# Hybrid decoder trunk on one core: own tiles for the retention's outputs, and raw weights in four slots of 4 KB instead of two of 8 KB

## The chip, the cores and the metric

The kernel runs on one core of a Trainium2 chip. The metric is the device time of one execution in microseconds (us), the median of several runs. The core has five engines with an instruction queue each: TensorE (PE, matmuls; PEld is its weight load), VectorE (DVE), ScalarE (ACT), GpSimd (POOL) and SyncE (SP, which here only issues DMA transfers). SBUF is the on-chip memory with 128 partitions, PSUM the accumulators that matmuls write, in banks of 128 x 512 float32 here. An engine works through its queue in order; between engines an instruction waits on semaphores.

## The reference

Two layers, each with a mixing part of three branches and a gated feed-forward part (FFN), in float32, for one sequence of 512 positions and 1024 channels. Cut to what matters here:

```
for l in range(2):
    h = rmsnorm(x, norm_mix_g[l])
    proj = h @ w_in[l]               # q, k, v of 4 attention heads; q, k, v, g of retention;
                                     # three conv streams; 3 x 1024 gate columns
    o_da  = rmsnorm(diff_attention(q, k, v, lam, bias)) * (1 - lam_init)
    o_ret = rmsnorm(retention(rq, rk, rv)) * silu(r_g)
    o_sc  = sc_b * causal_dwconv(sc_c * sc_x)
    gates = sigmoid(gate_pre + b_gate[l])
    y = gates0 * (o_da @ w_branch_da) + gates1 * (o_ret @ w_branch_ret) + gates2 * (o_sc @ w_branch_sc)
    x = x + y @ w_out[l]
    h = rmsnorm(x, norm_ffn_g[l])
    g_ff, u_ff = split(h @ w_ffn_in[l])          # 2 x 2816
    g_ff = causal_dwconv(g_ff)
    x = x + (silu(g_ff) * u_ff) @ w_ffn_out[l]
```

Differential attention subtracts a second softmax map, times lambda, from the first; a head has two maps of 64 channels each and values of 128.

## The kernel before

**Splitting.** Every float32 product runs as three matmuls of float32r parts (mm3, lines 159 to 161): high x high, high x low, low x high. So each weight tile is loaded raw by SP (load_w, line 137), its high half is made by ACT (line 150) and its low half by DVE (line 151, raw - high). Activations are split in the same way (lines 166 and 167; with a gain on them lines 169 and 170). The raw tiles share one tag of two slots of 8 KB per partition, the high and low halves of wide weights three slots each (HL). A load can be issued once an earlier tile of its slot has been split.

**Mixing.** "natural" computes projections with the positions on PSUM's partitions (four banks, tag "main", per head or pair): pnrqk and pnrvg for retention, pnh0 to pnh3 for the attention heads. "evacuate" (line 430) empties each bank of a head: a copy to nat, a square in place, v by split, a sum to msqk. The gates' and the convolution's projections (wt, tiles hi_t, lo_t; PSUM ptg and ptsc) run with channels on partitions; "gate" and "branch" make one gate and its branch product (pb) for a block d of 128 output channels. These, and the heads' projections, are the generator "filler". "weave" runs the steps of retention and attention and after each step asks the filler for work of a given cost (COVER), so that code order, with the waits for slots, sets the order of each engine's queue.

**Attention head h** makes q and k (transposes pt0, pt1, high and low parts in q, k, klz), then for each of four blocks i of 128 positions: scores (pS0, pS1, lines 487 and 488), bias and row minimum on DVE (line 492), exponential on ACT (493), combine (DVE), turn (transposes pT, line 511, split to aT), values (po, lines 523 and 524, with aT and v). At its end o is normalised, transposed (pto, line 284) and split to om. A name such as pT20L is pT of head 2, block 0; por00L and PT00L are the retention's.

**Slots.** q, k, v, rv, knh, knl, nat, rT, om, omr, y and act share tag "N", nine slots of 4 KB. The pool gives a new tile a free slot. In the program before, v of head 3 (v3) takes the slot of k of head 2 (k2) in both layers, whose last reader is the score matmul pS123. PSUM's main banks are four, shared by the heads' projections, gates, branches and the FFN.

**FFN.** The raw tile of one f (128 gate and 128 up columns) is 1 MB, in four blocks of 512 columns per partition. Group 0 (5 f's, "plain") uses the odd and the even blocks as gate and up weights. The other 17 f's of a layer ("seven") form seven block products in place of eight: fa (high and low of one block), s31 (two sums), s24 (two sums, from s31), fb (two blocks), each split on ACT and DVE, 84 matmuls of 256 columns. "rows" multiplies the group's activations by w_ffn_out (w2, PSUM p2) and adds to x. SP's issues are kept in program order only at the start, until all eight blocks of x are split.

## Time and profile before

| What | Value |
|---|---|
| median of 3 runs | 1548.77 us (1547.65 to 1552.67) |
| the profiled execution | 1550.88 us, span 1549.1 us |
| clock granted to PE, mean | 0.993 |
| PE busy | 1526.5 us (99%) |
| DVE, ACT busy | 1101.2 us (71%), 731.9 us (47%) |
| DMA | 148.54 MB, 96 GB/s over the span |

The span runs from the first to the last instruction of the profile; 1.8 us lie around it in that execution. A row of the timeline has the start in us, the duration, the engine, the line, the operation with its output and inputs, and in brackets the idle time of the engine ahead of it with what ended it. A window's row has, per engine, the busy time and the number of instructions, then the granted clock as a share of full speed, the busy share of the DMA engines and GB/s. Matmuls overlap, so the pace of PE is read from their starts, not from their durations.

### The profile page before, as it was taken

What the parts mean: (1) busy time and instruction counts of PE and PEld (TensorE: products, weight loads), DVE (VectorE), ACT (ScalarE), POOL (GpSimd) and SP (SyncE); (2) the same over time, 40 slices, a digit from 0 to 9 for tenths busy, and PEclk for the clock granted to TensorE, in tenths of its full rate; (3) what the DMA queues carried; (4) which work ended last, traced back from release to release, by engine and by line L of the source; (5) the groups of instructions that cost most, each with busy time, mean ns of one, the idle gap of its engine ahead of it and who ended that gap; (6) DMA issues with size and microseconds to landing.
All of it is one profiled execution on the core that took longest, in us unless ns stands there. A gap on an engine that the chain in (4) does not pass through costs nothing.

```text
span 1549.1 us, 21866 instructions
## 1 busy us (share of the span) xinstructions
PE 1526.5 (99%) x8510; PEld 1345.9 (87%) x8510; DVE 1101.2 (71%) x2040; ACT 731.9 (47%) x1304; POOL 14.1 (1%) x27
## 2 busy tenths in 40 slices
PE   9999989999999999999999999899999999999998
PEld 7899878888887999899789999688888879988997
DVE  7588776655569996597666887665546789957963
ACT  4456555433344564365425565453334446634641
POOL 1000000000000000000100000000000000000000
PEclk9999999999999999999999999899999999999999
DMA  5322222232221332331322222222323132224213
GB/s 188 116 103 63 88 74 84 85 98 96 98 88 55 142 110 69 136 137 55 129 82 92 72 89 72 68 81 90 102 76 123 68 110 110 92 84 165 96 45 106
DMA packets 43287, 148.54 MB, mean 96 GB/s; under 512 B 5703, under 2 KB 6102, under 8 KB 37552
## 3 DMA queue, kind: packets, MB, share of 16 engines
q1 hardware_dynamic: 41328, 143.37, 27.7%
q0 software_dynamic: 1856, 3.77, 0.7%
q8 instruction: 67, 1.10, 0.3%
q14 instruction: 36, 0.29, 0.1%
HBM read 145.01 MB, written 3.42 MB: 96 GB/s over the span
## 4 chain that ended last, share of the span: by engine, by line
PE 92%; DVE 3%; DMA 2%; ACT 2%; issue 1%; SPq 0%; ACTq 0%; DVEq 0%
PE pnrvgL L161 1%; PE pnrvgL L159 1%; PE pnrvgL L160 1%; PE pnrqkL L160 1%; PE pnrqkL L161 1%; PE pnrqkL L159 1%; PE pnh2L L161 1%; PE pnh2L L160 1%; PE pnh2L L159 1%; PE pnh1L L161 1%; PE pnh1L L160 1%; PE pnh1L L159 1%; PE pnh0L L160 1%; PE pnh0L L159 1%; PE pnh0L L161 1%
## 5 line engine op out<-in xcount | busy, mean ns | idle before, releaser
L150 ACT CAST hi_tL<-raw_tL 128x1024 fp32r<-128x1024 f32 x60 | 62.9, 1049 | 135.0 <-DMA raw_tL<-in_wt 18.3
L150 ACT CAST hi_w2L<-raw_w2L 128x640 fp32r<-128x640 f32 (+2 forms) x64 | 49.4, 781 | 97.8 <-DMA raw_w2L<-in_w 49.8
L151 DVE TENSOR_TENSOR lo_tL<-raw_tL,hi_tL 128x1024 fp32r<-128x1024 f32 x60 | 73.4, 1224 | 19.0 <-ACT hi_tL L150 18.8
L151 DVE TENSOR_TENSOR lo_w2L<-raw_w2L,hi_w2L 128x640 fp32r<-128x640 f32 (+2 forms) x64 | 56.2, 889 | 37.8 <-ACT hi_w2L L150 35.7
L150 ACT CAST hi_fbL<-raw_fL 128x1024 fp32r<-128x1024 f32 x34 | 35.7, 1051 | 26.2 <-PE p216L L160 11.7
L150 ACT CAST hi_oL<-raw_oL 128x1024 fp32r<-128x1024 f32 x16 | 16.9, 1054 | 58.1 <-issue 19.5
L151 DVE TENSOR_TENSOR lo_fbL<-raw_fL,hi_fbL 128x1024 fp32r<-128x1024 f32 x34 | 41.6, 1222 | 1.7 <-ACT hi_fbL L150 1.6
L150 ACT CAST hi_faL<-raw_fL 128x512 fp32r<-128x512 f32 x34 | 21.1, 622 | 30.9 <-DMA raw_fL<-in_wf 26.8
L151 DVE TENSOR_TENSOR lo_fuL<-raw_fL,hi_fuL 128x1024 fp32r<-128x1024 f32 x10 | 12.2, 1224 | 19.6 <-ACT hi_fuL L150 19.6
L150 ACT CAST hi_fuL<-raw_fL 128x1024 fp32r<-128x1024 f32 x10 | 10.5, 1051 | 31.2 <-PE pg0L L160 11.0
L151 DVE TENSOR_TENSOR lo_faL<-raw_fL,hi_faL 128x512 fp32r<-128x512 f32 x34 | 23.4, 689 | 0.3
L150 ACT CAST hi_nrvgL<-raw_nrvgL 128x1024 fp32r<-128x1024 f32 x8 | 8.4, 1051 | 31.5 <-PE pnrvgL L161 13.5
L150 ACT CAST hi_fgL<-raw_fL 128x1024 fp32r<-128x1024 f32 x10 | 10.5, 1054 | 24.1 <-issue 9.5
L151 DVE TENSOR_TENSOR lo_oL<-raw_oL,hi_oL 128x1024 fp32r<-128x1024 f32 x16 | 19.6, 1224 | 2.8 <-ACT hi_oL L150 2.8
L151 DVE TENSOR_TENSOR lo_nrvgL<-raw_nrvgL,hi_nrvgL 128x1024 fp32r<-128x1024 f32 x8 | 9.8, 1224 | 12.6 <-ACT hi_nrvgL L150 12.6
L151 DVE TENSOR_TENSOR lo_nh0L<-raw_nh0L,hi_nh0L 128x768 fp32r<-128x768 f32 x8 | 7.7, 958 | 13.4 <-ACT hi_nh0L L150 13.4
L150 ACT CAST hi_nrqkL<-raw_nrqkL 128x1024 fp32r<-128x1024 f32 (+1 forms) x9 | 8.6, 953 | 16.1 <-issue 11.1
L150 ACT CAST hi_bdL<-raw_bdL 128x512 fp32r<-128x512 f32 x16 | 9.9, 618 | 10.7 <-PE pb50L L160 2.2
L151 DVE TENSOR_TENSOR lo_nrqkL<-raw_nrqkL,hi_nrqkL 128x1024 fp32r<-128x1024 f32 (+1 forms) x9 | 9.9, 1105 | 7.0 <-ACT hi_nrqkL L150 7.0
L150 ACT CAST hi_nh0L<-raw_nh0L 128x768 fp32r<-128x768 f32 x8 | 6.7, 838 | 15.4 <-PE pnh0L L161 7.8
L151 DVE TENSOR_TENSOR lo_fgL<-raw_fL,hi_fgL 128x1024 fp32r<-128x1024 f32 x10 | 12.2, 1222 | 2.1 <-ACT hi_fgL L150 2.1
L150 ACT CAST hi_nh3L<-raw_nh3L 128x768 fp32r<-128x768 f32 x8 | 6.7, 835 | 14.0 <-PE ptg17L L160 7.3
(8455 smaller groups left out, 5985.4 us busy)
## 6 DMA issues: line engine op xcount, KB each, us to landing
raw_fL<-in_wf SPq DMA_DIRECT2D x44, 1024.0 KB, 4.8
raw_tL<-in_wt SPq DMA_DIRECT2D x60, 512.0 KB, 3.3
raw_w2L<-in_w SPq DMA_DIRECT2D x32, 320.0 KB, 2.9
raw_oL<-in_wo SPq DMA_DIRECT2D x16, 512.0 KB, 3.3
raw_w2L<-in_w SPq DMA_DIRECT2D x16, 512.0 KB, 3.5
raw_nrvgL<-in_wr SPq DMA_DIRECT2D x8, 512.0 KB, 3.2
raw_bdL<-in_wda SPq DMA_DIRECT2D x16, 256.0 KB, 2.6
raw_w2L<-in_w SPq DMA_DIRECT2D x16, 256.0 KB, 2.6
```

The source lines that it names most:

```text
L150: A.copy(h, raw)
L151: V.tensor_tensor(w, raw, h.bitcast(F32), ALU.subtract)
L159: T.matmul(o, a[0], b[0], start=start, stop=False, skip_group_check=more)
L160: T.matmul(o, a[0], b[1], start=False, stop=False, skip_group_check=more)
L161: T.matmul(o, a[1], b[0], start=False, stop=stop, skip_group_check=more)
```

## The change

Three things. The two outputs of retention, omr0 and omr1, get tiles of their own in the layer's mixing pool instead of slots of tag "N". The raw tag has four slots of 4 KB (16 KB as before). And the FFN's loads are made of two halves: "plain" loads the gate blocks and the up blocks apart, "seven" loads two neighbouring blocks at a time, so that s31's broadcast sum over blocks of both halves becomes two sums of 512 columns. The layout in memory is the same, so a plain half comes in pieces of 2 KB.

```diff
--- before.py
+++ after.py
@@ -131,10 +131,10 @@
         return i
 
     def load_w(src, name):
-        n = src.shape[1]
+        n = int(np.prod(src.shape[1:]))
         with tc.high_priority():
-            raw = wp.tile([P, n], F32, tag="raw", bufs=2, name="raw_" + name, padded_shape=[P, 2 * D])
-            ordered(nc.sync.dma_start(raw, src))
+            raw = wp.tile([P, n], F32, tag="raw", bufs=4, name="raw_" + name, padded_shape=[P, D])
+            ordered(nc.sync.dma_start(raw if len(src.shape) == 2 else raw.rearrange("p (b n) -> p b n", b=src.shape[1]), src))
         return raw
 
     def split_w(raw, name):
@@ -643,7 +643,7 @@
             yield
             yield
             ps = transposes(lambda st: o[:, st * P : (st + 1) * P], f"ptor{p}{L}")
-            om[4 + p] = split2(ps, pairN(f"omr{p}{L}"), pt[:, G_RET : G_RET + 1])
+            om[4 + p] = split2(ps, mp.tile([P, 2, S], F32R, name=f"omr{p}{L}"), pt[:, G_RET : G_RET + 1])
             yield
 
 
@@ -770,9 +770,9 @@
             split(flat(t), flat(X[k][:, 0, 3:7]), flat(X[k][:, 1, 3:7]))
 
         def plain(f):
-            raw = load_w(wf[l, f], f"f{L}{f}").rearrange("p (b n) -> p b n", n=S)
+            both = wf[l, f].rearrange("p (b n) -> p b n", n=S)
             ps = main(f"pg{f}{L}")
-            project(xg, ps, split_w(raw[:, 1::2], f"fg{L}{f}"))
+            project(xg, ps, split_w(load_w(both[:, 1::2], f"fg{L}{f}"), f"fg{L}{f}"))
             if not norm:
                 norm.append(norm_x(f"f{L}")[1])
             padt = pads[f % 2]
@@ -782,20 +782,20 @@
             conv(c, padt, lambda t: pt[:, wc + t : wc + t + 1], pt[:, FF_B + f : FF_B + f + 1])
             A.activation(c, c, AF.Silu)
             ps = main(f"pu{f}{L}")
-            project(xg, ps, split_w(raw[:, 0::2], f"fu{L}{f}"))
+            project(xg, ps, split_w(load_w(both[:, 0::2], f"fu{L}{f}"), f"fu{L}{f}"))
             u = temp(f"u{f}{L}")
             V.tensor_tensor(u, ps, norm[0], ALU.mult)
             V.tensor_tensor(u, u, c, ALU.mult)
             return split2(u, pairN(f"act{f}{L}"))
 
         def seven(f):
-            raw = load_w(wf[l, f], f"f{L}{f}")
-            r4 = raw.rearrange("p (b n) -> p b n", n=S)
-            a11, a12 = r4[:, 1], r4[:, 3]
+            upper, lower = [load_w(wf[l, f, :, b * D : (b + 1) * D], f"f{b}{L}{f}") for b in range(2)]
+            a21, a11, a22, a12 = upper[:, :S], upper[:, S:], lower[:, :S], lower[:, S:]
             with tc.high_priority():
-                w11 = split_w(raw[:, S : 2 * S], f"fa{L}{f}")
+                w11 = split_w(a11, f"fa{L}{f}")
                 s31 = fp.tile([P, 2, S], F32, tag="sum", name=f"s31{f}{L}", bufs=2)
-                V.tensor_tensor(s31, r4[:, 0:1].broadcast_to([P, 2, S]), r4[:, 1:3], ALU.add)
+                V.tensor_tensor(s31[:, 0], a21, a11, ALU.add)
+                V.tensor_tensor(s31[:, 1], a21, a22, ALU.add)
                 h31, l31 = slotX(f"h31{f}{L}"), slotX(f"l31{f}{L}")
                 split(s31, h31, l31)
                 s24 = fp.tile([P, 2, S], F32, tag="sum", name=f"s24{f}{L}", bufs=2)
@@ -803,7 +803,7 @@
                 V.tensor_tensor(s24[:, 1], s24[:, 0], a12, ALU.add)
                 h24, l24 = slotX(f"h24{f}{L}"), slotX(f"l24{f}{L}")
                 split(s24, h24, l24)
-                w2212 = split_w(raw[:, 2 * S : 4 * S], f"fb{L}{f}")
+                w2212 = split_w(lower, f"fb{L}{f}")
             w22, w12 = [tuple(t[:, b * S : (b + 1) * S] for t in w2212) for b in range(2)]
 
             def product(o, w, b, start, stop):
```

The places where the order of instructions differs follow, from the program before and from the changed one.

PE, layer 0, from the end of head 3's projection (pnh3L03 is its fourth bank) on; po02 are the values of head 2, pS0 and pS1 its scores, pto1 head 1's output. Before, pT20 is directly ahead of po02, and nine more rows of head 2 follow the last one shown ahead of pb22, the first branch product:

```order
L161 MATMUL pnh3L03_2044<-hi_nh3L06_2200,xs7mL0_233 128x384
L511 MATMUL pT20L0_2152<-ident_79,s020L0_2030 128x128
L523 MATMUL po02L0_2192<-v2L0_1562,aT20L0_2154 128x256
L524 MATMUL po02L0_2192<-v2L0_1562,aT20L0_2154 128x128
L284 MATMUL pto1L0_2248<-ident_79,o1L0_1543 128x128 x4
L487 MATMUL pS022L0_2257<-k2L0_1934,q2L0_1933 128x384
L488 MATMUL pS022L0_2257<-klzL0_122,q2L0_1933 128x384
L487 MATMUL pS122L0_2258<-k2L0_1934,q2L0_1933 128x384
L488 MATMUL pS122L0_2258<-klzL0_122,q2L0_1933 128x384
L511 MATMUL pT21L0_2271<-ident_79,s021L0_2144 128x128 x2
```

The same place of PE in the changed program; pT20 stands seven rows ahead of the first one shown:

```order
L161 MATMUL pnh3L02_2043<-hi_nh3L06_2200,xs7mL0_233 128x384
L159 MATMUL pnh3L03_2044<-hi_nh3L06_2200,xs6mL0_230 128x384
L160 MATMUL pnh3L03_2044<-lo_nh3L06_2201,xs6mL0_230 128x384
L161 MATMUL pnh3L03_2044<-hi_nh3L06_2200,xs6mL0_230 128x384
L159 MATMUL pnh3L03_2044<-hi_nh3L06_2200,xs7mL0_233 128x384
L160 MATMUL pnh3L03_2044<-lo_nh3L06_2201,xs7mL0_233 128x384
L161 MATMUL pnh3L03_2044<-hi_nh3L06_2200,xs7mL0_233 128x384
L523 MATMUL po02L0_2192<-v2L0_1562,aT20L0_2154 128x256
L524 MATMUL po02L0_2192<-v2L0_1562,aT20L0_2154 128x128
L159 MATMUL pb22L0_2300<-oms0L0_1034,hi_b2L02_2296 128x512
L160 MATMUL pb22L0_2300<-oms0L0_1034,hi_b2L02_2296 128x512
```

So pT20 has 13 matmuls of pnh3 between it and po02, and pb22 follows po02 at once. Behind pb22 come a gate of 24 matmuls, the next branch product and five matmuls of another gate, and only then pto1, pS022 and pS122. Layer 1 has the same order as layer 0 here.

ACT, layer 0, the same stretch. Before, from aT20 up to the first copies into v3 (line 169), which stand behind the exponential s023 of block 3:

```order
L166 CAST aT20L0_2154<-pT20L0_2152 128x128
L433 ACTIVATE pnh3L03_2044<-pnh3L03_2044 128x256
L525 COPY o2L0_2020<-po02L0_2192 128x128
L527 ACTIVATE po02L0_2192,mso2L0_2022<-o2L0_2020,zs2L0_2021 128x128
L493 ACTIVATE s022L0_2263,z22L0_2256<-s022L0_2263,mn022L0_2264 128x384
L493 ACTIVATE s122L0_2267,z22L0_2256<-s122L0_2267,mn122L0_2268 128x384
L166 CAST aT21L0_2274<-pT21L0_2271 128x256
L493 ACTIVATE s023L0_2361,z23L0_2354<-s023L0_2361,mn023L0_2362 128x512
L525 COPY o2L0_2020<-po02L0_2192 128x128
L169 ACTIVATE v3L0_2039<-pnh3L00_2041,rmL0_298 128x128
L169 ACTIVATE v3L0_2039<-pnh3L01_2042,rmL0_298 128x128
```

In the changed program, from the conversion of a gate's weights on:

```order
L150 CAST hi_tL026_2409<-raw_tL026_2407 128x1024
L432 COPY nat3L0_2038<-pnh3L00_2041 128x256
L433 ACTIVATE pnh3L00_2041<-pnh3L00_2041 128x256
L166 CAST aT20L0_2154<-pT20L0_2152 128x128
L169 ACTIVATE v3L0_2039<-pnh3L00_2041,rmL0_298 128x128
L432 COPY nat3L0_2038<-pnh3L01_2042 128x256
L433 ACTIVATE pnh3L01_2042<-pnh3L01_2042 128x256
L169 ACTIVATE v3L0_2039<-pnh3L01_2042,rmL0_298 128x128
```

Each copy into v3 now follows the square of its bank. On DVE the low half of v3 and the sum msqk3 of the first three banks follow aT20's low half, which has one lo_t ahead of it.

SP, at the start. Before, the third load of retention's projection waits behind four constants:

```order
L198 DMA x3_85<-in_xT 128x512
L204 DMA par1_111<-in_par 128x140
L205 DMA gtab_t_113<-in_gtab 128x32
L206 DMA mask_t_90<-in_mask 128x128
L380 DMA ropeL0_126<-in_rope 128x512
L137 DMA raw_nrqkL02_182<-in_wr 128x1024
L198 DMA x4_86<-in_xT 128x512
```

In the changed program it follows x3 at once, and the constants stand behind the last load of that projection:

```order
L198 DMA x3_85<-in_xT 128x512
L137 DMA raw_nrqkL02_182<-in_wr 128x1024
L198 DMA x4_86<-in_xT 128x512
L198 DMA x5_87<-in_xT 128x512
L198 DMA x6_88<-in_xT 128x512
L198 DMA x7_89<-in_xT 128x512
L137 DMA raw_nrqkL04_222<-in_wr 128x1024
```

Over the whole program PE has the same 8510 matmuls, DVE 34 sums more, and SP 44 loads more.

## The prediction

> **What bounds the kernel now.** I read the page's busy shares and its chain first, then the waits of PE, then the granted clock in slices.

> ```profile
> PE 1526.5 (99%) x8510; PEld 1345.9 (87%) x8510; DVE 1101.2 (71%) x2040; ACT 731.9 (47%) x1304; POOL 14.1 (1%) x27
> PE 92%; DVE 3%; DMA 2%; ACT 2%; issue 1%; SPq 0%; ACTq 0%; DVEq 0%
> ```

> PE is on 92% of the chain that ended last, and the change leaves all its matmuls in place. So only time in which PE stands, or runs at a lower clock, can be won. The waits of PE (total, times, longest) name these places:

> ```profile
> PE po02L L523 <- ACT aT20L L166: 3.9, 2, 2.0
> PE pto1L L284 <- DVE o1L L544: 2.7, 2, 1.4
> PE pb22L L159 <- DVE msqk3L L435: 2.2, 2, 1.4
> PE por00L L617 <- ACT PT00L L166: 1.8, 1, 1.8
> PE po02L L524 <- DVE aT20L L167: 1.4, 2, 0.7
> PE pnrqkL L159 <- ACT hi_nrqkL L150: 1.3, 2, 1.1
> ```

> Four of the six stand together, in one hole per layer, behind pT20. The windows over the two holes and over what follows each (PE busy, matmuls, granted clock, DMA share, GB/s) give their size:

> ```profile
> 206.19:219.00 12.81, 6.74 (x26) 0.87 0.19 56
> 219.00:226.00 7.00, 7.00 (x31) 1.00 0.00 0
> 971.16:984.03 12.87, 8.07 (x25) 0.67 0.15 56
> 984.03:992.00 7.97, 7.97 (x25) 0.68 0.00 0
> ```

> The second row is PE at full pace: 31 matmuls of 512 columns in 7.00 us, 0.226 each. Narrow ones are shorter; these transposes start 0.11 apart:

> ```profile
> 77.15 0.27 PE L284 MATMUL ptr1L<-ident,rr1L 128*128 128x128 f32 x1
> 77.26 0.27 PE L284 MATMUL ptr1L<-ident,rr2L 128*128 128x128 f32 x1
> ```

> In layer 0's hole lie 10 transposes (1.1 us), 8 score matmuls of at most 512 columns (under 1.6 us by widths) and 6 value matmuls (0.7 us, my estimate between the two prices), then pb22. That is 3.4 us of work in 12.81, so **9.4 us lost**. Layer 1 loses 12.87 - 3.4 = 9.5, and behind it 25 matmuls took 7.97 us where 25 x 0.226 = 5.7 would do: 2.3 more at a clock of 0.68, together **11.8**.

> Why does nothing fill the hole? These rows of PE, ACT and DVE, in order of time, say it:

> ```profile
> 205.84 0.33 PE L160 MATMUL pnh3L<-lo_nh3L,xs7mL 128*128 128x384 f32 x1
> 206.01 0.34 PE L161 MATMUL pnh3L<-hi_nh3L,xs7mL 128*128 128x384 f32 x1
> 206.19 0.27 PE L511 MATMUL pT20L<-ident,s020L 128*128 128x128 f32 x1
> ...
> 216.55 0.40 PE L488 MATMUL pS123L<-klzL,q2L 128*128 128x512 f32 x1
> ...
> 219.00 0.50 PE L159 MATMUL pb22L<-oms0L,hi_b2L 128*128 128x512 f32 x1 [1.44 <-DVE msqk3L L435]
> ```
> ```profile
> 217.32 1.14 ACT L169 ACTIVATE v3L<-pnh3L,rmL 128x128 fp32r<-128x128 f32 x4
> ```
> ```profile
> 218.53 0.41 DVE L435 TENSOR_REDUCE msqk3L<-pnh3L 128x4 f32<-128x256 f32 x1
> ```

> Head 3's projection (pnh3) ended ahead of 206.19, but its copies into v3 start at 217.32, right behind head 2's last score pS123. In this program v3 lies in the slot of k2 (tag "N", nine slots), which pS123 still reads. Until v3 is copied the four banks of pnh3 are not free, and all that could run beside head 2's chain (pb22, ptg19 and the gates behind them) needs such a bank.

> **The change part by part. Own tiles for omr0 and omr1.** They leave tag "N", so two more slots are free there. In the changed program v3 takes the slot of nat2, last read by the transposes pt12, some 90 rows of PE ahead of pT20, and each v3 copy stands right behind its bank's square. pb22, gates and two more branch products now lie between the steps of head 2. PE then pays the 3.4 us and the fill, which is work it did later anyway: -9.4 - 11.8 = -21.2.

> Not all of it goes. The ACT half of aT20 still has the conversion of a gate's weights (hi_tL) ahead of it, and DVE's half has lo_tL; pT20 has only 13 matmuls of pnh3 between it and po02. Bounds for po02: nothing, and the 2.0 + 0.7 us of the waits above, per layer. I take 0.6, nearer to nothing, since its cover of 13 x 0.17 = 2.2 us (206.01 - 205.84 each) comes near the 2.7 that lacked. That leaves -21.2 + 1.2 = **-20.0**.

> **Four raw slots of 4 KB.** A raw load can be issued while three others wait to be split. The waits of SP's queue show how long issues waited for a slot until now:

> ```profile
> SPq L137 <- DVE lo_tL L151: 172.3, 34, 21.1
> ```

> Nearly all of that hides behind PE. Where it shows is the wait for PT00 of the list, in layer 0 only:

> ```profile
> 50.33 0.96 DVE L151 TENSOR_TENSOR lo_nh0L<-raw_nh0L,hi_nh0L 128x768 fp32r<-128x768 f32 x1 [2.46 <-ACT hi_nh0L L150]
> ```
> ```profile
> 65.79 3.14 SPq L137 DMA_DIRECT2D raw_tL<-in_wt  x2
> ```
> ```profile
> skew<-line POOLq DMA_DIRECT2D x1, 1280.0 KB, 19.5
> ```
> ```profile
> 73.24 1.05 ACT L150 CAST hi_tL<-raw_tL 128x1024 fp32r<-128x1024 f32 x1 [5.92 <-DMA raw_tL<-in_wt]
> ...
> 76.18 0.62 ACT L166 CAST PT00L<-rd00L 128x512 fp32r<-128x512 f32 x1 [0.51 <-DVE rd00L L601]
> ```
> ```profile
> 75.00:78.00 3.00, 1.18 (x11) 1.15 (x10) 3.00 (x9) 2.46 (x9) 0.80 (x1) 0.96 0.46 148
> 78.00:81.00 3.00, 3.00 (x13) 2.61 (x11) 2.94 (x9) 2.95 (x8) 0.00 (x0) 0.50 0.85 333
> ```

> A transposed projection's weights, issued at 65.79, came while the skewed bias table was being written (19.5 us to landing); ACT, in order, stood 5.92 us with R0 and PT00 behind that conversion, PE idled 1.8 us and then ran at half clock, 0.50 in the second window. That took 1.8 + 3.4 / 2 = 3.5 us (I put the stretch of half clock at 3.4 us, from the starts of PE's rows). With four slots the two wt loads need only the slots that the second split of nh0 frees (50.33 + 0.96 us), 14 us earlier, which covers the 5.92. I take **-3.3**; the ends are 0 and -3.5.

> [...]

> At the start the third load of rqk waited for a slot too, behind the constants and the rope table (SP, then ACT, then PE):

> ```profile
> 7.06 0.33 SPq L137 DMA_DIRECT2D raw_nrqkL<-in_wr  x1
> ```
> ```profile
> 12.39 1.04 ACT L150 CAST hi_nrqkL<-raw_nrqkL 128x1024 fp32r<-128x1024 f32 x1 [0.70 <-DMA raw_nrqkL<-in_wr]
> ```

> Now it follows x3 with nothing to wait for. ACT can win its 0.70 us at most, because work stands ahead of the conversion: **-0.6**, between 0 and -0.7.

> **Halves of f.** The first seven of group 1 waited for a load of 1 MB, and PE had 30.59 us of 31 around it:

> ```profile
> 508.50 1.23 DVE L798 TENSOR_TENSOR s315L<-raw_fL 128x1024 f32<-128x1024 f32 x1 [1.69 <-DMA raw_fL<-in_wf]
> ...
> 510.24 0.68 DVE L802 TENSOR_TENSOR s245L<-s315L,raw_fL 128x512 f32<-128x512 f32 x1
> ...
> 510.85 1.22 DVE L151 TENSOR_TENSOR lo_fbL<-raw_fL,hi_fbL 128x1024 fp32r<-128x1024 f32 x1
> ```
> ```profile
> 496.00:527.00 31.00, 30.59 (x188) 27.35 (x187) 25.73 (x32) 14.54 (x21) 0.00 (x0) 1.00 0.48 164
> 527.00:558.00 31.00, 31.00 (x261) 31.00 (x260) 30.89 (x42) 20.05 (x34) 0.00 (x0) 1.00 0.29 108
> 558.00:589.00 31.00, 31.00 (x261) 31.00 (x260) 29.86 (x40) 19.93 (x36) 0.00 (x0) 1.00 0.24 81
> ```

> The halves take slots that free earlier; the 0.41 us may go: **-0.4**, between 0 and -0.4.

> The price is on DVE: s31 is two instructions in place of one, in 34 sevens. By durations that is 2 x 0.68 - 1.23 = 0.13 each. By starts a 512-wide one takes 0.61 (510.24 to 510.85) and the wide one 1.14 (508.50 to the next start at 509.64), so 0.08. Over 34 it is 2.7 to 4.4 us of DVE. PE (columns: PE, PEld, DVE, ACT, POOL) was full in the last two windows; DVE had 1.14 us left in the third, which hides three sevens' 0.4, and 0.11 in the second, which does not. About six sevens per layer run so close behind group 1's start: 12 x 0.08 = **+1.0**, between 0 and 4.4.

> The 44 added loads cost SP an issue of 0.33 us each, on a queue that is waiting for slots anyhow; each half is a transfer of 512 KB. The plain f's need one such half per 24 x 0.226 = 5.4 us of PE, and the page's gate loads of that size land in less:

> ```profile
> raw_fL<-in_wf SPq DMA_DIRECT2D x44, 1024.0 KB, 4.8
> raw_tL<-in_wt SPq DMA_DIRECT2D x60, 512.0 KB, 3.3
> ```

> Their smaller pieces of 2 KB are not in the trace as weights: between 3.3 and 4.8 us I take the upper end, still under 5.4, and cost them at nothing. If that cover failed, 20 halves at 0.5 us would be 10 us.

> The sum against the profiled 1550.88 us: -20.0 - 3.3 - 0.6 - 0.4 + 1.0 = -23.3, so 1527.6. That execution stood 2.1 us above the median of the runs, so the median should be **1525.5**.

> **The rivals.** *The hole comes back in part.* Head 2's first value matmul meets ACT and DVE as busy as before, and po02's waits return: 2.7 us a layer, and with them a window of half clock, another 1.7. That is 8.8 for both, 1.2 of it in the sum: 1525.5 + 7.6 = 1533. For it speaks that the conversions still stand ahead of aT20; against it, that the scores of head 2 now come earlier too.

> *Only the own tiles act.* The loads go out earlier but land against the table's writing all the same: 1525.5 + 3.3 + 0.6 + 0.4 = 1530. Against it: those 14 us are twice what the load then took.

> *The split shows in full.* DVE is last in all sevens: 4.4 - 1.0 more, 1529. [...]

> *It does not do what it says.* v3 meets another late reader and the hole stays: 1548.8 with the small terms about even, within 1544 to 1553.

> *Slower.* The second half of s31 waits for the lower load, in order, with the rest of a seven behind it on DVE. If that load lands 4.8 - 3.3 = 1.5 us later than the upper one and no slot is ahead, a seven takes DVE 9.6 (29.86 x 10.0 / 31) + 0.1 + 1.5 = 11.2 us against PE's 84 x 31 / 261 = 10.0: +1.2 x 34 = 41, and 1525.5 + 41 = 1567. It turns the change into a loss from 23.3 / 34 = 0.7 us per seven on. Against it: with four slots a seven's halves are loaded while the one before it is split, some 10 us ahead.

> **How the numbers follow.** Forecast 0.74, hole back in part 0.11, only the own tiles 0.05, the split in full 0.04, no effect 0.02, slower 0.04. The first four are faster by over 0.3% (4.6 us, about what a measurement of this kernel can tell from no change): 0.94; same 0.02; slower 0.04. The range: at best all bounds hold (-1.2 - 0.2 - 0.1 - 1.0 from the forecast) and a few waits of PE for w2 weights shrink, 1519; at worst the hole is back in part with some of the split, 1536. That leaves out 0.06 of the cases and what I have mis-sized.

> **What would show it.** In the changed profile the windows behind pT20 should be full at a clock of 1.00, v3's copies should start within two microseconds of their bank's last matmul, the half clock at 78 should be gone, hi_nrqkL's wait should be under 0.5 us, and s31's halves should be near 0.68 with DVE under PE in each window of the sevens. The prediction is wrong if po02 still waits over 1 us, if a new wait of PE over 1 us appears in the sevens or the plain f's, or if the clock falls anywhere new.

## The result, and the profile after

| | before | changed |
|---|---|---|
| median of 4 runs | 1550.24 us (1547.65 to 1552.67) | 1524.91 us (1524.34 to 1525.94) |
| the profiled execution | 1550.88 us, span 1549.1 us | 1524.34 us, span 1522.6 us |
| mean granted clock of that execution | 0.993 | 1.0 |

The ratio is 0.9838 with a 95% interval of 0.9818 to 0.9857, a gain of 25.3 us; the forecast was 1525.5. The page of the changed kernel opens like this (busy time and share of the span, then the chain that ended last):

```profile
PE 1513.1 (99%) x8510; PEld 1338.8 (88%) x8510; DVE 1103.6 (72%) x2074; ACT 733.6 (48%) x1304; POOL 14.1 (1%) x27
PE 94%; DVE 3%; DMA 1%; issue 1%; ACT 0%; SPq 0%; ACTq 0%; DVEq 0%
```

PE does the same 8510 matmuls in 13.4 us less of busy time, and the span is 26.5 us shorter. A part of the 13.4 is half clock that is gone (20.7 us of before's span stand at a clock of 0.50, none of the changed kernel's); another part is that a matmul that stands alone between waits is counted with its whole duration (in layer 0's hole 6.74 us were busy with the 3.4 us of work that the prediction counts there). DVE has the 34 added sums (2074 for 2040) and 2.4 us more to do. The waits of PE (total, times, longest):

```profile
PE p204L L159 <- ACT hi_w2L L150: 1.6, 2, 0.8
PE ps_warm L190 <- POOL ones L184: 1.1, 1, 1.1
PE pnrqkL L159 <- ACT hi_nrqkL L150: 0.9, 2, 0.6
PE pa5L L159 <- ACT pad L819: 0.8, 2, 0.6
```

Everything that waited behind pT20, and the wait for PT00, is gone from the list; pa5 on ACT's pad is new. The stretches of 12.81, 12.87 and 7.97 us behind pT20 that were shown of before, taken from where pT20 now stands (198.85 and 953.41), and two slices around the former wait for PT00 (PE busy, matmuls, clock, DMA share, GB/s):

```profile
198.85:211.66 12.81, 12.81 (x65) 1.00 0.23 84
953.41:966.28 12.87, 12.87 (x66) 1.00 0.23 84
966.28:974.25 7.97, 7.97 (x38) 1.00 0.30 102
70.00:73.00 3.00, 3.00 (x19) 1.00 0.62 208
73.00:76.00 3.00, 3.00 (x26) 1.00 0.27 48
```

Where 26 and 25 matmuls stood, 65 and 66 run, at full clock.

### The profile page after: what moved, and what is told of

The parts are those of the page before. It is cut to its first block, busy times and chain, and to the rows that moved or that the text cites. A ratio compares the mean times of both kernels' runs of the same rounds, so it can differ in the third digit from the quotient of the medians.

```text
span 1522.6 us, 22066 instructions
## 1 busy us (share of the span) xinstructions
PE 1513.1 (99%) x8510; PEld 1338.8 (88%) x8510; DVE 1103.6 (72%) x2074; ACT 733.6 (48%) x1304; POOL 14.1 (1%) x27
## 4 chain that ended last, share of the span: by engine, by line
PE 94%; DVE 3%; DMA 1%; issue 1%; ACT 0%; SPq 0%; ACTq 0%; DVEq 0%
DMA raw_f1L<-in_wf 1%; PE pnrvgL L161 1%; PE pnrvgL L159 1%; PE pnrvgL L160 1%; PE pnrqkL L160 1%; PE pnrqkL L161 1%; PE pnrqkL L159 1%; PE pnh2L L161 1%; PE pnh2L L159 1%; PE pnh3L L160 1%; PE pnh3L L161 1%; PE pnh1L L161 1%; PE pnh2L L160 1%; PE pnh3L L159 1%; PE pnh1L L160 1%
## 5 line engine op out<-in xcount | busy, mean ns | idle before, releaser
L150 ACT CAST hi_tL<-raw_tL 128x1024 fp32r<-128x1024 f32 x60 | 62.9, 1049 | 115.3 <-issue 19.8
L150 ACT CAST hi_w2L<-raw_w2L 128x640 fp32r<-128x640 f32 (+2 forms) x64 | 49.5, 783 | 87.2 <-PE p214L L160 10.4
L151 DVE TENSOR_TENSOR lo_tL<-raw_tL,hi_tL 128x1024 fp32r<-128x1024 f32 x60 | 73.4, 1223 | 15.9 <-ACT hi_tL L150 15.6
L151 DVE TENSOR_TENSOR lo_w2L<-raw_w2L,hi_w2L 128x640 fp32r<-128x640 f32 (+2 forms) x64 | 56.0, 885 | 28.8 <-ACT hi_w2L L150 28.8
L150 ACT CAST hi_fbL<-raw_f1L 128x1024 fp32r<-128x1024 f32 x34 | 35.7, 1050 | 38.6 <-PE pa8L L160 6.8
L151 DVE TENSOR_TENSOR lo_fbL<-raw_f1L,hi_fbL 128x1024 fp32r<-128x1024 f32 x34 | 41.4, 1219 | 5.2 <-ACT hi_fbL L150 5.0
L150 ACT CAST hi_oL<-raw_oL 128x1024 fp32r<-128x1024 f32 x16 | 16.9, 1054 | 58.1 <-issue 25.2
L150 ACT CAST hi_faL<-raw_f0L 128x512 fp32r<-128x512 f32 x34 | 21.1, 621 | 26.9 <-DMA raw_f0L<-in_wf 8.6
L151 DVE TENSOR_TENSOR lo_fuL<-raw_fuL,hi_fuL 128x1024 fp32r<-128x1024 f32 x10 | 12.2, 1222 | 19.6 <-ACT hi_fuL L150 19.6
L151 DVE TENSOR_TENSOR lo_faL<-raw_f0L,hi_faL 128x512 fp32r<-128x512 f32 x34 | 23.3, 684 | 3.5 <-ACT hi_faL L150 3.5
L150 ACT CAST hi_fuL<-raw_fuL 128x1024 fp32r<-128x1024 f32 x10 | 10.5, 1050 | 31.1 <-issue 17.5
L150 ACT CAST hi_nrvgL<-raw_nrvgL 128x1024 fp32r<-128x1024 f32 x8 | 8.4, 1051 | 29.6 <-PE pnrvgL L161 13.5
L150 ACT CAST hi_fgL<-raw_fgL 128x1024 fp32r<-128x1024 f32 x10 | 10.5, 1054 | 24.1 <-issue 16.0
L151 DVE TENSOR_TENSOR lo_oL<-raw_oL,hi_oL 128x1024 fp32r<-128x1024 f32 x16 | 19.6, 1224 | 2.8 <-ACT hi_oL L150 2.8
L151 DVE TENSOR_TENSOR lo_nrvgL<-raw_nrvgL,hi_nrvgL 128x1024 fp32r<-128x1024 f32 x8 | 9.8, 1220 | 12.5 <-ACT hi_nrvgL L150 12.5
L151 DVE TENSOR_TENSOR lo_nh0L<-raw_nh0L,hi_nh0L 128x768 fp32r<-128x768 f32 x8 | 7.7, 956 | 13.1 <-ACT hi_nh0L L150 13.1
L150 ACT CAST hi_bdL<-raw_bdL 128x512 fp32r<-128x512 f32 x16 | 9.9, 619 | 12.6 <-issue 5.3
L150 ACT CAST hi_nrqkL<-raw_nrqkL 128x1024 fp32r<-128x1024 f32 (+1 forms) x9 | 8.5, 951 | 15.0 <-issue 13.9
L151 DVE TENSOR_TENSOR lo_nrqkL<-raw_nrqkL,hi_nrqkL 128x1024 fp32r<-128x1024 f32 (+1 forms) x9 | 9.9, 1105 | 6.1 <-ACT hi_nrqkL L150 6.1
L150 ACT CAST hi_nh0L<-raw_nh0L 128x768 fp32r<-128x768 f32 x8 | 6.7, 838 | 15.2 <-PE pnh0L L161 7.8
L151 DVE TENSOR_TENSOR lo_fgL<-raw_fgL,hi_fgL 128x1024 fp32r<-128x1024 f32 x10 | 12.2, 1220 | 2.2 <-ACT hi_fgL L150 2.2
L150 ACT CAST hi_nh3L<-raw_nh3L 128x768 fp32r<-128x768 f32 x8 | 6.7, 838 | 11.3 <-PE ptg16L L160 5.3
## 6 DMA issues: line engine op xcount, KB each, us to landing
raw_tL<-in_wt SPq DMA_DIRECT2D x60, 512.0 KB, 3.3
raw_f0L<-in_wf SPq DMA_DIRECT2D x34, 512.0 KB, 3.7
raw_f1L<-in_wf SPq DMA_DIRECT2D x34, 512.0 KB, 3.7
raw_oL<-in_wo SPq DMA_DIRECT2D x16, 512.0 KB, 3.3
raw_w2L<-in_w SPq DMA_DIRECT2D x16, 512.0 KB, 3.5
raw_fgL<-in_wf SPq DMA_DIRECT2D x10, 512.0 KB, 4.0
raw_fuL<-in_wf SPq DMA_DIRECT2D x10, 512.0 KB, 4.0
```

What stands on the lines that cost most here:

```text
L150: A.copy(h, raw)
L151: V.tensor_tensor(w, raw, h.bitcast(F32), ALU.subtract)
```

## The experiments

Each run has its own runs of the kernel before beside it, on the same chip: median 1551.73 us for the first four, 1549.59 for the next four, 1550.46 for the last two.

**The own tiles alone (own_only).** The kernel before, with this edit:

```diff
-            om[4 + p] = split2(ps, pairN(f"omr{p}{L}"), ...)
+            om[4 + p] = split2(ps, mp.tile([P, 2, S], F32R, name=f"omr{p}{L}"), ...)
```

> Only the two own tiles for omr, raw slots and f loads as before. If v3's slot is the whole cause of the two holes, the waits behind pT20 (po02, pto1, pb22) fall under 1 us in all and the time by 20 us (18 to 22) to about 1530; the wait for PT00 (1.8 us), the half clock behind it and the 1.1 us of hi_nrqkL stay. If the gates that fill the hole need the deeper raw loads as well, half of the holes comes back and the gain is about 10 us.

Measured: 1526.9 us (1526.23, 1526.49, 1527.31 and 1531.35), ratio 0.9842 (0.9825 to 0.986), 24.8 us. That is more than the 20 expected, with PT00's wait still in place, as the profiled run, the one of 1531.35 us, shows (the row from its waits, then slices from its windows):

```profile
PE por00L L617 <- ACT PT00L L166: 1.9, 1, 1.9
```
```profile
75.00:78.00 3.00, 1.56 (x11) 0.94 0.66 169
78.00:81.00 3.00, 3.00 (x12) 0.50 0.77 311
81.00:84.00 3.00, 3.00 (x9) 0.50 0.40 122
```

Half clock lasts through two slices here, where before had one; why two is open. The other three runs had a mean clock of 1.000 against this one's 0.997, and were 4 to 5 us shorter: by the mean clock, for they have no trace, the same kernel met the half clock behind that wait in one execution of four. The hole itself is gone: no wait of PE on po02, pto1 or pb22 is left in the list. From pnh3's first matmul to po0's, the stretch that holds the hole, PE took 199.9 and 202.3 us in the two layers before and takes 189.9 in both here, 22.3 us less. Of the 4.8 us beyond 20, that is 2.3: the 1.2 for po02 that did not come, and holes that were dearer by 1.1. I put about 1.7 (an estimate, half of the 3.4 us that half clock lasted there before) down to the half clock behind PT00 that three of the runs were spared, and 0.9 to before's median, which here lay above the execution of 1550.88 us. Before itself varies: its 26 runs in the first two batches lie between 1548.25 and 1555.23 us, with a mean clock of 0.989 in the three longest and of 0.990 to 0.995 in the others, which fits holes that cost a varying amount of half clock.

**Raw slots and halves alone (raw_only).** The changed kernel with omr back in tag "N" (the edit above the other way round).

> The changed kernel with omr back in tag N: four raw slots and halves of f alone. By my sum 4.3 us less the price of the split, 3 to 4.5 us faster than before; the holes behind pT20 stay at over 9 us each, PT00's wait and the half clock near 78 are gone. If deeper loads alone let the gates run beside head 2, the holes shrink and the gain is 10 us or more.

Measured: 1543.93 us (1543.33 to 1544.72), ratio 0.9946 (0.9931 to 0.9961), 7.8 us. PT00's wait is gone, as expected. But the hole behind pT20 shrank too, to 10.96 us from 12.81:

```profile
201.28 0.27 PE L511 MATMUL pT20L<-ident,s020L 128*128 128x128 f32 x1
203.02 0.38 PE L523 MATMUL po02L<-v2L,aT20L 128*128 128x256 f32 x1 [1.46 <-ACT aT20L L166]
...
212.24 0.50 PE L159 MATMUL pb22L<-oms0L,hi_b2L 128*128 128x512 f32 x1 [0.59 <-DVE msqk3L L435]
```

po02 and pto1 wait 0.5 us less in each layer than before (1.46 for 1.99 in layer 0), and pb22 0.9 less in layer 0 (0.59 for 1.44) and no less in layer 1. From pnh3's first matmul to po0's PE takes 2.0 us less in each layer. So 4 of the 7.8 us that the raw slots give by themselves lie in a hole that the own tiles remove anyhow. Why the waits are shorter with the slots of "N" as before was not tried apart; ACT's queue ahead of aT20 is in another order.

**One tile for v3 (v3_own).** The kernel before, with a tile of its own for v of head 3 and omr left where it was:

```diff
-            v = pairN(f"v{h}{L}")
+            v = pairN(f"v{h}{L}") if h < H - 1 else mp.tile([P, 2, S], F32R, name=f"v{h}{L}")
```

> The kernel before with one tile of its own, for v of head 3, and omr left in tag N. If what counts is that v3 waits for k2's last reader, this does what the two omr tiles did: 18 to 21 us faster, v3's copies right behind their banks. If it is the omr tiles themselves, or two more free slots, that matter, the holes stay and the time is that of before within 2 us.

Measured: 1531.1 us (1530.64 to 1532.14), ratio 0.9864 (0.9849 to 0.9879), 20.6 us. Omr was not touched, so v3's slot is the cause of the holes. Two short waits are left behind pT20 in layer 0 (the timeline of PE):

```profile
206.42 0.47 PE L159 MATMUL pb22L<-oms0L,hi_b2L 128*128 128x512 f32 x1 [0.23 <-DVE nto1L L234]
...
208.45 0.47 PE L159 MATMUL ptg19L<-xs0mL,hi_tL 128*128 128x512 f32 x1 [0.41 <-DVE fo1L L239]
```

Here pb22 stands right behind pT20, with no matmuls of pnh3 between, so the emptying of the banks is late by those 0.2 to 0.4 us. In the changed kernel the last banks of pnh3 cover it. From pnh3's first matmul to po0's PE takes 191.8 and 191.6 us here against own_only's 189.9 twice, which is 3.5 of the 4.2 us between the two runs.

**The split by itself (s31_split).** The kernel before, raw tiles of 1 MB as they were:

```diff
-                V.tensor_tensor(s31, r4[:, 0:1].broadcast_to([P, 2, S]), r4[:, 1:3], ALU.add)
+                V.tensor_tensor(s31[:, 0], r4[:, 0], r4[:, 1], ALU.add)
+                V.tensor_tensor(s31[:, 1], r4[:, 0], r4[:, 2], ALU.add)
```

> The kernel before with s31 as two sums of 512 columns from the same raw tile of 1 MB: the price of the split by itself. My sum has +1.0 us (PE full, DVE 0.08 more for each of 34); if DVE is last in all sevens +4.4 us; if DVE has slack everywhere 0, with PE's waits in the sevens as before.

Measured: 1551.95 us, ratio 1.0001 (0.9989 to 1.0013): no cost that the times can show, but the interval reaches from -1.7 to 2.0 us, so they exclude the 4.4 and not the 1.0. In these windows over the sevens PE stays full while DVE has next to nothing left (columns: PE, PEld, DVE, ACT, POOL, then clock, DMA share, GB/s):

```profile
520.00:551.00 31.00, 31.00 (x260) 31.00 (x260) 29.39 (x41) 18.46 (x31) 0.00 (x0) 1.00 0.28 103
551.00:582.00 31.00, 31.00 (x261) 31.00 (x260) 30.86 (x45) 20.39 (x35) 0.00 (x0) 1.00 0.30 103
```

A DVE that is 30.86 of 31 us busy need not be late: PE waits for nothing in these windows, so DVE works ahead of it, and the split takes from that lead. Just ahead of them, where the lead is being built, PE has a wait that before does not have, 0.3 us in each layer:

```profile
PE pb6L L159 <- ACT h316L L166: 0.6, 2, 0.3
```

h316 is made from the second seven's s31. From pa5's first matmul to pa14's, the sevens of group 1, PE takes 140.7 us in both layers here, and took 140.6 and 139.7 before: 1.1 us more, all of it in layer 1. That is one execution of each kernel.

The same run has one more thing to show. Its wait for PT00 is 1.7 us long, and the clock did not fall:

```profile
72.00:75.00 3.00, 2.06 (x14) 1.00 0.11 43
75.00:78.00 3.00, 2.23 (x16) 1.00 0.89 267
78.00:81.00 3.00, 3.00 (x19) 1.00 0.54 214
```

**Both parts again, and the depth of the slots (after_again, slots3, slots2).** The changed kernel as it is, and with this edit to three and to two slots:

```diff
-            raw = wp.tile([P, n], F32, tag="raw", bufs=4, ...)
+            raw = wp.tile([P, n], F32, tag="raw", bufs=3, ...)
```

> The changed kernel beside its own two parts, on the same footing. Own tiles alone gave 24.8 us, raw slots and halves alone 7.8 us. If the parts are independent, both together give 32 us; if the raw slots' part overlaps with the hole that the own tiles remove (raw slots alone cut the two holes by some 4 us, and PT00's half clock came only in some runs), 25 to 27 us.

> The changed kernel with three raw slots of 4 KB. If depth counts only where a load is late, the loads of a seven still come one seven ahead and PT00's load goes out at the third split of nh0, in time: 0 to 5 us slower than with four slots. If each load's depth shows, 10 us or more.

> The changed kernel with two raw slots of 4 KB: the slower rival made true. The lower half of a seven can only be loaded once the lower half before it is split, 3.7 us to landing, and s31's second half waits for it in DVE's order: some 2 to 3 us per seven less the 0.4 us of slack, 34 sevens, so 40 to 100 us slower than with four slots. If the loads are hidden anyhow, within 5 us.

| | median us (runs) | mean clock | ratio to before, 95% |
|---|---|---|---|
| after_again | 1525.29 (1525.07 to 1525.39) | 0.999 to 1.0 | 0.984 (0.9824 to 0.9856) |
| slots3 | 1525.5 (1525.27 to 1526.2) | 0.999 to 1.0 | 0.9843 (0.9828 to 0.9857) |
| slots2 | 1548.23 (1545.23 to 1554.04) | 0.993 to 0.998 | 0.9993 (0.998 to 1.0006) |

Both parts together give 24.3 us here, not 32: they overlap. Three slots do what four do. Two give 23 us back, nearly all that the change had won, though less than the 40 to 100 expected. The waits of PE with two slots:

```profile
PE pb15L L159 <- DVE x L849: 5.3, 2, 2.7
PE pa6L L159 <- ACT hi_faL L150: 3.2, 2, 2.1
PE por00L L617 <- ACT PT00L L166: 1.7, 1, 1.7
```

and DVE at s31, two rows from group 1 and two from its waits:

```profile
523.63 0.69 DVE L797 TENSOR_TENSOR s318L<-raw_f0L 128x512 f32<-128x512 f32 x1 [0.70 <-DMA raw_f0L<-in_wf]
...
534.62 0.69 DVE L797 TENSOR_TENSOR s319L<-raw_f0L 128x512 f32<-128x512 f32 x1 [0.36 <-DMA raw_f0L<-in_wf]
```
```profile
DVE s3114L L797 <- DMA raw_f0L<-in_wf: 6.8, 2, 3.6
DVE s317L L797 <- DMA raw_f0L<-in_wf: 4.1, 2, 2.1
```

The wait is not the one expected. It is mostly s31's first sum (L797) that waits, for the upper load (raw_f0), and not the second for the lower: 0.4 to 0.7 us in the two sevens shown, but 2.1 in s317 and 3.6 in s3114, with which group 2 starts. All that the s31 and s24 of the 34 sevens wait for loads is some 30 us, against 5.5 in the changed kernel, and a part of it hides behind DVE's lead. PE's last matmul starts 22.3 us later than in the changed kernel's profile. Of that 18.0 us lie in the sevens, most of it where a group starts (pa6 and pa5, pb15 and pa14) and 0.5 to 0.7 at each of pa11 and pa12 in group 1's middle; 2.8 lie ahead of pnh1, where the wait for PT00 is back.

**Holes put in (stalls, stalls_short).** The changed kernel, with the first matmul of each output product made to wait for the product before it, through a chain of short instructions. The core of the edit in stalls_short (in stalls the chain goes over a column on DVE and a conversion on ACT):

```diff
+                late = mp.tile([P, P], F32R, tag="late", name=f"late{e}{L}", bufs=2)
+                V.scalar_tensor_tensor(late, ps[:, :P], 0.0, raw[:, :P], ALU.mult, ALU.add)
+                for _ in range(STALL[l][e - 1]):
+                    V.scalar_tensor_tensor(late, late.bitcast(F32), 0.0, raw[:, :P], ALU.mult, ALU.add)
...
+                mm3(ps, (late if e and not k else w[0][:, sl], w[1][:, sl]), yk, k == 0, k == KT - 1)
```

> The changed kernel with 14 holes made on purpose between the output products: the first matmul of each waits for a chain of 1 to 13 short DVE instructions and an ACT conversion that start from the product before, holes of some 1 to 3.5 us with 5.4 us of full work between. If a hole beyond a fixed length brings half clock, one length parts the holes with it from those without. If it is a matter of where a hole falls in a running window of 3.4 us, holes of one length (1.5 to 2.5 us) come with and without half clock, and the mean clock differs from run to run. The time is longer by the holes, 14 x 2 = 28 us, plus 1.7 us for each window at half clock.

> 14 holes between the output products again, now by DVE alone (1 to 5 short instructions in a chain), 1.2 to 2.4 us each. If half clock needs a hole beyond a fixed length between 1.9 and 2.55 us, the short ones have none and the longest all. If it depends on where the hole falls in a running window, holes of about 2 us come both with and without it, and those under 1.2 us without.

Measured: 1615.31 and 1600.22 us. The holes came out longer than meant, since other work of DVE and ACT slipped into the chains, but their lengths spread well. Two holes of one length in stalls, 2.39 us of idle each (PE's timeline, then five windows of 3.41 us: the first holds most of the first hole, the third and fourth the second):

```profile
377.62 0.50 PE L160 MATMUL po1L<-y0L,late1L 128*128 128x512 f32 x1 [2.39 <-ACT late1L L745]
...
387.37 0.50 PE L160 MATMUL po2L<-y0L,late2L 128*128 128x512 f32 x1 [2.39 <-ACT late2L L745]
```
```profile
375.62:379.03 3.41, 1.41 (x6) 1.00 0.17 23
379.03:382.44 3.41, 3.41 (x10) 0.50 0.35 131
382.44:385.86 3.42, 2.54 (x11) 1.00 0.00 0
385.86:389.27 3.41, 1.90 (x8) 1.00 0.27 79
389.27:392.68 3.41, 3.41 (x16) 1.00 0.18 74
```

The first brought half clock, the second, of the same length, none. All holes of these two runs, with those of PT00 in the profiled runs:

| idle of PE | holes | with half clock behind them |
|---|---|---|
| 1.0 us (stalls_short) | 2 | 0 |
| 1.7 to 1.9 us (PT00: before, own_only, v3_own, s31_split, slots2) | 5 | 3 |
| 2.4 us | 4 | 3 |
| 2.8 to 5.8 us | 22 | 22 |

No single length of a hole parts them. In the two runs with holes put in, the stretch at half clock can begin 1.4 us after PE has taken up work again (377.62, and the clock falls at 379.03), and lasts for 7 to 14 matmuls of 0.43 us, 3 to 6 us.

**Less memory (lean).** One own tile, omr0, and three raw slots, 8 KB per partition less than the changed kernel:

```diff
-            raw = wp.tile([P, n], F32, tag="raw", bufs=4, ...)
+            raw = wp.tile([P, n], F32, tag="raw", bufs=3, ...)
-            om[4 + p] = split2(ps, mp.tile([P, 2, S], F32R, name=f"omr{p}{L}"), ...)
+            om[4 + p] = split2(ps, (mp.tile([P, 2, S], F32R, name=f"omr{p}{L}") if p == 0 else pairN(f"omr{p}{L}")), ...)
```

> One own tile (omr0) in place of two, and three raw slots in place of four: 8 KB per partition less than the changed kernel. If one more free slot is enough to keep v3 out of k2's slot, and three raw slots do what four do, the time is that of the changed kernel within 1.5 us, 1525. If the second tile or the fourth slot counted, a hole of some 10 us is back in each layer, 1545.

Measured: 1525.19 us (1525.19 to 1525.7), ratio 0.9841 (0.9826 to 0.9855): the time of the changed kernel. One more free slot in tag "N" is enough to keep v3 out of k2's slot: in layer 0 v3's copies start at 198.7 us, k2's last reader pS123 only at 219.5, and in layer 1 the last of v3's copies starts at 958.3, pS123 at 974.8.

## Why the prediction was right, and where its terms were off

**Own tiles, -20.0: right, and the largest term.** The cause was the one named (v3_own), and the own tiles alone gave 24.8 us (own_only). The residual of 1.2 us for po02 did not come: its wait is gone. The holes themselves were worth 22.4 us between the two profiled executions (pnh3's first matmul to po0's, 199.9 and 202.3 us down to 189.9 twice), for the 21.2 of the sum. The cover was thin, though. These rows of the changed kernel, of ACT, DVE and PE in turn, show it:

```profile
199.54 0.26 ACT L166 CAST aT20L<-pT20L 128x128 fp32r<-128x128 f32 x1
199.70 0.36 ACT L169 ACTIVATE v3L<-pnh3L,rmL 128x128 fp32r<-128x128 f32 x1
```
```profile
199.16 1.22 DVE L151 TENSOR_TENSOR lo_tL<-raw_tL,hi_tL 128x1024 fp32r<-128x1024 f32 x1
200.29 0.15 DVE L237 SCALAR_TENSOR_TENSOR nto1L<-fo1L 128x4 f32<-128x4 f32 x1
200.36 0.28 DVE L167 TENSOR_TENSOR aT20L<-pT20L,aT20L 128x128 fp32r<-128x128 f32 x1
200.56 0.34 DVE L170 SCALAR_TENSOR_TENSOR v3L<-pnh3L,rmL,v3L 128x128 fp32r<-128x128 f32 x1
200.82 0.41 DVE L435 TENSOR_REDUCE msqk3L<-pnh3L 128x4 f32<-128x256 f32 x1
```
```profile
201.22 0.28 PE L523 MATMUL po02L<-v2L,aT20L 128*128 128x256 f32 x1
201.33 0.22 PE L524 MATMUL po02L<-v2L,aT20L 128*128 128x128 f32 x1
201.39 0.45 PE L159 MATMUL pb22L<-oms0L,hi_b2L 128*128 128x512 f32 x1
```

The low half of aT20 is done at 200.64, 0.6 us ahead of po02, and the bank that pb22 takes is free at 201.23, 0.16 us ahead of it. The rival in which the hole comes back in part was that close, and lo_t is what stood ahead of aT20 on DVE.

**Raw slots at PT00, -3.3: the mechanism right, the size half a matter of chance.** The first of the wt loads goes out at 46.61 in place of 58.42 (SP, before and then changed):

```profile
58.42 10.51 SPq L137 DMA_DIRECT2D raw_tL<-in_wt  x3
```
```profile
46.61 10.84 SPq L137 DMA_DIRECT2D raw_tL<-in_wt  x3
```

ACT converts at 67.53 and has PT00 done at 71.54, where before it began PT00 at 76.18:

```profile
67.53 1.05 ACT L150 CAST hi_tL<-raw_tL 128x1024 fp32r<-128x1024 f32 x1 [2.76 <-PE pnh0L L161]
...
70.93 0.61 ACT L166 CAST PT00L<-rd00L 128x512 fp32r<-128x512 f32 x1
```

The failed part of the step is "3.4 / 2" of half clock as a fixed price of 1.8 us of idle. One execution had been read as a rule; the wait itself, 1.7 to 1.9 us, is the certain part, and the half clock came behind it in three of five profiled runs. The wait lies right at the edge, where in these traces 1.8 us of idle in a window brought half clock and 1.7 did not. From pnh0's first matmul to pnh1's PE took 45.6 us before and 42.0 in the changed kernel, so between these two executions the term was 3.6.

**Start, -0.6: about right.** ACT's wait of 0.70 us is gone. PE's wait on hi_nrqk is 0.9 us in all for 1.3, and pnh0's first matmul starts at 54.7 to 54.8 us in the profiles of after, after_again and raw_only and at 55.0 to 56.0 in those of before, own_only, v3_own and s31_split: 0.3 to 1.3 us.

**Halves of f, -0.4: the wrong sign.** The failed step is "the halves take slots that free earlier; the 0.41 us may go". Layer 0 won 0.2 us there (30.77 of 31 us in the window that held 30.59), but a new wait came in both layers, 0.8 us in this profile, 1.8 in after_again's and 2.4 in raw_only's. The longest in after_again's is 1.1 us: by the prediction's own sign, a new wait over 1 us in the sevens, this step is wrong there. A window of all engines, then ACT, then PE:

```profile
500.50:531.50 31.00, 30.77 (x257) 30.57 (x256) 29.91 (x43) 17.78 (x30) 0.00 (x0) 1.00 0.32 109
```
```profile
500.55 1.05 ACT L150 CAST hi_fbL<-raw_f1L 128x1024 fp32r<-128x1024 f32 x1 [2.23 <-DMA raw_f1L<-in_wf]
501.50 0.61 ACT L150 CAST hi_faL<-raw_f0L 128x512 fp32r<-128x512 f32 x1
502.02 0.36 ACT L819 COPY pad<-pa5L 128x256 f32<-128x256 f32 x1
```
```profile
502.44 0.39 PE L159 MATMUL pa5L<-X0L,h245L 128*128 128x256 f32 x1 [0.23 <-ACT pad L819]
```

ACT stands 2.23 us for a lower half of f, in order, with the emptying of pa5 behind it. It is the mechanism of the slower rival, a half that comes late in an in-order queue, on ACT in place of DVE and only at a group's start. slots2 shows late halves over both groups of sevens: 18.0 us, 0.5 per seven on average, against the 1.2 per seven (41 us) that the rival had priced, and mostly through the upper half in place of the lower.

**The split, +1.0: not settled by the times.** s31_split measured 1.0001 of before, with an interval that holds +1.0 and excludes the 4.4 of the rival. Its trace shows 1.1 us more in group 1, at the first sevens, and none in the windows behind them, where DVE had next to no slack. So it looks to be DVE's lead over PE that decides, and not the slack of a window, as the prediction had it. In the changed kernel pb6 does not wait, and all that its group 1 loses stands at pa5. By durations the price is there: s315's two sums take 0.69 and 0.68 us in s31_split, where before's one took 1.23, 0.15 more; in the time of the kernel it could not be told from nothing.

**The plain halves, nothing: right.** They land in 4.0 us, between the 3.3 and 4.8 that bounded them, and PE waits for none.

**The sum.** 23.3 us forecast, 25.3 and 24.3 measured. Between the two profiled executions the last matmul of PE starts 26.8 us earlier. By the starts of PE's rows 1.3 us of that lie ahead of pnh0 (forecast 0.6), 3.6 from pnh0 to pnh1, with PT00 (3.3), 22.4 from pnh3 to po0 (20.0), and -0.4 in group 1 from pa5 to pa14, where the halves and the split act (0.4 - 1.0 = -0.6); what is left is -0.1. So the term that was mis-sized is that of the holes, by 2.4 us.

In the medians the terms were not independent, as the sum had taken them: the holes are worth 25 us alone, all else 8 us alone, and 24 to 25 together. What the raw slots add beside own tiles is not shown clear of noise: own_only's three runs at full clock took 1526.2 to 1527.3 us and after_again's 1525.1 to 1525.4, but on different chips, and against its own runs of before own_only gained 24.8 us and after_again 24.3.

That the median came out within 0.6 us of the forecast is in part luck. The gain was 2 us over the forecast one, and the 2.1 us taken off for the profiled execution came from a median of three runs; with the fourth, 1550.24 us, they would have been 0.6, and the forecast 1526.9.

## What to carry to other kernels

When PE stands with work queued behind it, look for the tile whose slot the blocked copy needs, and who reads that slot last: one extra slot of 4 KB was worth 21 us by itself here (v3_own), and 25 with the raw slots (lean), because four PSUM banks and all the filler hung on it. Price a hole of TensorE by its idle time, and half clock behind it by how much of that idle can fall into one window of 3.41 us: in these traces under 1.7 us cost none, with one exception, and over 1.8 us nearly always did. Removing the holes also narrowed the runs, from 1546.46 to 1555.23 us down to 1524.34 to 1525.94. Prefetch depth paid up to the load that was late and no further (two slots 1548, three 1525.5, four 1525.3), and two gains that end at the same wait did not add (24.8 and 7.8 us apart, 24.3 together).

## What had not been expected of the hardware

Half clock can set in while PE is already working again (the first slow matmul behind the 2.39 us hole of stalls came 1.55 us after the restart), and holes of 2.39 us did and did not bring it in one execution, by where the edges of the 3.41 us windows cut them. The runs of the kernel before, spread over 9 us, probably had this as a source: their mean clock ran from 0.989 to 0.996, and their longest had the lowest.
